# Accumulator banks of a two-layer hybrid trunk: four fixed pairs for the whole program in place of pools per stage

## The chip, the cores and the metric

One core of a Trainium2 chip runs the whole program in one launch. The metric is the device time of one execution in microseconds (us); a kernel's time is the median of its runs. The core's engines are TensorE (PE: matrix products and transposes, which write into accumulator banks), VectorE (DVE), ScalarE (ACT), GpSimd (POOL) and SyncE (SP, which issues most transfers). Each engine works through its own list of instructions in order, and engines wait for each other through semaphores that count finished instructions.

## The reference: what is computed

Two layers of a trunk over 512 latent tokens and 128 context tokens of width 1024. Cut to what matters:

```python
def _layer(x, mod, p, lam_init, ctx):
    sh1, sc1, g1, sh2, sc2, g2 = mod
    h = _rmsnorm(x, p['norm1']) * (1.0 + sc1) + sh1
    m, new_ctx = _mixer(h, p, lam_init, ctx)
    x = x + g1 * m
    h = _rmsnorm(x, p['norm2']) * (1.0 + sc2) + sh2
    x = x + g2 * _conv_ffn(h, p)
    return x, new_ctx
```

The mixer is one input projection, split among a recurrent head group (RG-LRU with convolution, gates and scans in two directions), grouped-query attention and differential attention, and one output projection over the three. The ConvFFN is an up projection to 2 x 2816 channels, a width-3 convolution, silu(g) * a, and a down projection. The conditioning rows (sh, sc, g) are products of the condition with a 1024 x 6144 matrix. A last norm follows.

## The kernel before

Every large product is made of three products of float32r parts (high by high, high by low, low by high: `mm3`, lines 347 to 350). Two kinds of loop carry them:

- `stat_mm` (line 595): weights stand still, tokens stream. One accumulator is two banks from `pb2` (line 260), one for each part of the 640 tokens, filled one after the other. The up projection (`up_pair`, 22 times a layer, two accumulators each, tile `uacc`) and the recurrent group's inputs (`lacc`) use it. Behind the second bank, `conv` copies both to SBUF with three ACT instructions (lines 1371 to 1373).
- `tok_products` (line 1302) and `proj_group` (line 617): tokens stand still, weights stream; one bank for each of five token tiles (`tacc`, `acc`). The output and down projections empty a bank by `residual`: DVE multiplies it with the gate (line 1298) and adds it to x (1299).

Smaller uses of banks: transposes of normed tokens (`nT`, `norm_b` and `norm_c`, lines 550 to 564: a token tile fills two banks, and DVE scales four blocks of the one while ACT scales four blocks of the other), of q and k (`qT`, `kT`, `dT`), gate products (`gacc`, line 706), the context's own attention (`cS`, `cPTp`), the conditioning products (`ada`, eight chunks into one bank), and in the attention stage scores (`S`), transposed probabilities (`PT`) and value products (`PV`).

Memory for accumulators is eight banks of 512 float32 a partition. Before, `psum_mode` opens pools for a stage: eight single banks (`pb`) in all stages but attention, and there three tiles of two banks (`ps`, for S and PT) and two single ones (`pb`: PV, dT, ada, adaT). At a change of stage it closes the pools and opens others on the same banks. Each call of `pb` or `ps` makes a new tile of its own, and the pool gives out its places in turn; the first instruction on a place waits for the readers of the tile that held it.

The order of the work is written by hand: the program is recorded in the order of the Python calls. `Flow` (line 55) puts small follow-up steps into the stream of products by planned times, and in the attention stage `Plan` (line 98) picks the next task by keys, planned durations and counts of free places (`ROOM`, line 104: three pairs and two single banks). Neither asks the pools; waits are added afterwards, between instructions that touch the same tile.

Of the kernel before, what the change touches and what calls it, by code (L numbers as in the profile page):

```python
# [2 lines left out]

# [8 lines left out]
F32 = mybir.dt.float32  # L12
# [204 lines left out]
def hybrid_kernel(ctx: ExitStack, tc: tile.TileContext, i, o):  # L217
# [22 lines left out]
    def tslot(name, n=644, dt=F32):  # L240
        return tp.tile([128, 644], dt, tag="t", name=name)[:, :n]

    psum, mode = ctx.enter_context(ExitStack()), {}

    def psum_mode(double, single):

        psum.close()
        for key, n in (("ps", double), ("pb", single)):
            if n:
                mode[key] = psum.enter_context(tc.tile_pool(name=key, bufs=n, space=bass.MemoryType.PSUM))  # L250

    psum_mode(0, 8)

    def ps(name, dt=F32):
        return mode["ps"].tile([128, 1024], dt, tag="ps", name=name)

    def pb(name, dt=F32):
        return mode["pb"].tile([128, 512], dt, tag="pb", name=name)

    def pb2(name, cut=CH):  # L260

# [221 lines left out]
    def ada_gen(l, u):  # L483

        acc = pb("ada")
        for k in range(KD):
            while not split_done:
                split_next()
            n = split_done.pop(0)
            for j in range(4):  # L490
                pe.matmul(acc[32 * j:32 * j + 32, :], lhsT=cc[:, k].rearrange("p a b -> p (a b)"), rhs=raws[n][:, j, :],
                          start=(k == 0), stop=(k == KD - 1), tile_position=(0, 32 * j))
            load_to(n + 2)
            if k == KD - 2:
                bias, ar, src = tslot("abias", 512), tslot("arow", 512), i["ada_b"]
                sp.dma_start(out=bias, in_=bass.AP(tensor=src.tensor, offset=src.offset + l * 6 * D + u * 2048,
                                                   ap=[[512, 4], [0, 32], [1, 512]]))
            fl.now += 1100
            yield
        dve.tensor_tensor(out=ar, in0=acc, in1=bias, op=ALU.add)  # L500
        if u:
            d = drp.tile([2, 1024], F32, tag=f"gate{u}", name=f"gate{u}")
            for j in range(2):
                r = 32 * (j + (0 if u == 1 else 2))
                sp.dma_start(out=d[:, j * 512:(j + 1) * 512], in_=ar[r:r + 2, :])
            res["g", l, u] = d
        yield
        pt = pb("adaT")
        for b in range(4):
            pe.transpose(pt[:, b * 128:b * 128 + 128], ar[:, b * 128:b * 128 + 128], ident)  # L510
        c = smp.tile([128, 2, 4, 4], F32, tag=f"cm{u}", bufs=2, name=f"cm{u}")
        for r in range(2):
            dve.tensor_copy(out=c[:, r], in_=pt.rearrange("p (b j q) -> p q j b", b=4, j=4)[:, r])
        res["c", l, u] = c.rearrange("p r j b -> p r (j b)")
# [117 lines left out]
    def mixer(l, hh, hl, first=None):  # L632
# [268 lines left out]
        def d_stack(df, dest, c0, order, jp):  # L901
# [17 lines left out]
            def out():  # L919
                for e in range(2):  # L920
                    dve.tensor_copy(out=dest[e][0:96, :, c0:c0 + 128],
                                    in_=f32(box[0][0:96, e * 256:e * 256 + 256].rearrange("p (h c) -> p h c", h=2)))
                pending[jp] -= 1

            return lo, tr, out

# [183 lines left out]
        else:  # L1110
            for m in range(2):
                lru_in(m, first[m])
        rope_tables_()
        for c in range(2):
            for d in range(2):
# [15 lines left out]
        for m in (2, 3):  # L1131
            w, acc = weights(), pb2("lacc")
            for c in range(2):
                stat_mm(acc, w, hh, hl, c, step=888)
                lru_in(m, acc, c)
        wait("a")
        wait(0)
        psum_mode(3, 2)
# [4 lines left out]
        def unit(kind, h, q):  # L1143
# [27 lines left out]
            def exp(c):  # L1171
                box["P"].append(tslot("P", T))
                act.activation(out=box["P"][c].rearrange("p (a b) -> p a b", a=2), in_=view(c), func=ACTF.Exp,  # L1173
                               bias=box["nm", c], accum_out=box["den"][:, c:c + 1])

            def recip():
                den = box["den"]
# [17 lines left out]
            def out():  # L1195
                if not e:
                    PTs[kind, p, q] = half("PT")[:, 0:1280].rearrange("p (k c) -> p k c", k=5)
                act.activation(out=PTs[kind, p, q][:, :, e * 128:e * 128 + 128],
                               in_=box["pt"][:, 0:T].rearrange("p (k c) -> p k c", k=5), func=ACTF.Copy)

            return dict(score=score, top=top, exp=exp, recip=recip, norm=norm, comb=comb, tr=tr, out=out)

        def values_of(kind, p, q):
# [19 lines left out]
            def out():  # L1223
# [4 lines left out]
                else:  # L1228
                    if not dn:
                        dn.append(v2(half("dn"), T))  # L1230
                    dst = dn[0][:, p, c0:c0 + nn]
                act.activation(out=dst, in_=box[0][:, 0:nn], func=ACTF.Copy)

            def hi():
                m = mixed[2 + p] = v2(half("mix", F32R), T)
# [257 lines left out]
    for t in range(NT):  # L1493
# [10 lines left out]
        out=cc,  # L1504
        in_=cps[:, 0:16].rearrange("p (r k) -> p k r", r=2).unsqueeze(2).to_broadcast([128, KD, 16, 2]),
    )
    rps1 = pb("rps1")
    pe.transpose(rps1[:, 0:32], rows1, ident[0:32, 0:32])
    dve.tensor_copy(out=cols1, in_=rps1[:, 0:32])
    sc1 = small("sc1", 8)  # L1510
    dve.tensor_scalar(out=sc1, in0=cols1[:, R_AB + 8:R_AB + 16], scalar1=1.0, scalar2=None, op0=ALU.add)
    act.activation(out=identr, in_=ident, func=ACTF.Copy)
# [18 lines left out]
    for g in range(2):  # L1531
# [3 lines left out]
        for e in range(2):  # L1535
            dve.tensor_copy(out=xT[2 * g + e][:, :, L:T], in_=pt[:, e * 256:e * 256 + 256].rearrange("p (k c) -> p k c", k=2))

    h = ([], [])

    def modulate(p):  # L1540
# [51 lines left out]
    for l in range(DEPTH):  # L1592
# [5 lines left out]
        if not more:  # L1598
            sps = pb("sps")
            pe.transpose(sps[0:8, 0:128], stc, ident)  # L1600
            srow = tslot("srow", 128)[0:8]
            dve.tensor_copy(out=srow, in_=sps[0:8, 0:128])
            sp.dma_start(out=o["new_lru_state"].rearrange("a l d (c p) -> (a l d c) p", p=128), in_=srow)
        ffn(l, h[0], h[1], res["g", l, 2], AB1(l + 1) if more else None, h2)
        h = h2
# [52 lines left out]
```

## Time and profile before

| | us |
|---|---|
| median of 3 runs | 1647.7 |
| lowest, highest | 1647.31, 1648.01 |
| the profiled execution | 1648.27 |
| its span, first to last instruction | 1646.5 |
| PE busy in the span | 1596.4 |
| DVE, ACT, POOL busy | 942.4, 725.4, 347.6 |

The profile is of one execution, and durations come from it. Stages by the span's time: start 0 to 47, projections of layer 0 up to 180, attention to 309, output projection and norm to 383, feed-forward to 858 (its end holds the norm before layer 1), projections of layer 1 to 989, attention to 1109, output projection and norm to 1184, feed-forward and last norm to 1646.5. Two matrix products that follow each other overlap in the records: a product of 320 columns is recorded as some 310 ns, and the next starts 150 ns after it.

### The profile page before, as it was taken

What the parts mean: (1) busy time and instruction counts of PE and PEld (TensorE: products, weight loads), DVE (VectorE), ACT (ScalarE), POOL (GpSimd) and SP (SyncE); (2) the same over time, 40 slices, a digit from 0 to 9 for tenths busy, and PEclk for the clock granted to TensorE, in tenths of its full rate; (3) what the DMA queues carried; (4) which work ended last, traced back from release to release, by engine and by line L of the source; (5) the groups of instructions that cost most, each with busy time, mean ns of one, the idle gap of its engine ahead of it and who ended that gap; (6) DMA issues with size and microseconds to landing.
All of it is one profiled execution on the core that took longest, in us unless ns stands there. A gap on an engine that the chain in (4) does not pass through costs nothing. (4 is left out here: it accounts for less than half of the span.)

```text
span 1646.5 us, 25389 instructions
## 1 busy us (share of the span) xinstructions
PE 1596.4 (97%) x10070; PEld 1395.2 (85%) x10070; DVE 942.4 (57%) x1548; ACT 725.4 (44%) x1500; POOL 347.6 (21%) x746
## 2 busy tenths in 40 slices
PE   6999999999999999999999999999999999999998
PEld 4787777789999889999887787777899998899986
DVE  5785867555555334555467677875655553345544
ACT  4745677644333212333247357784433331133321
POOL 5162243122111000111052613420411100011101
PEclk9999999999999999999999999999999999999999
DMA  9222365411312321222212214443112232121312
GB/s 330 68 89 83 128 214 202 170 52 52 103 52 92 114 77 52 78 78 78 102 36 70 80 58 134 151 141 127 41 63 77 77 128 78 45 84 52 103 65 90
DMA packets 99435, 161.04 MB, mean 98 GB/s; under 512 B 10670, under 2 KB 69222, under 8 KB 94196
## 3 DMA queue, kind: packets, MB, share of 16 engines
q1 hardware_dynamic: 98068, 158.00, 28.7%
q8 instruction: 79, 1.29, 0.3%
q0 software_dynamic: 1040, 1.14, 0.2%
q14 instruction: 40, 0.33, 0.1%
q10 hardware_dynamic: 208, 0.28, 0.0%
HBM read 155.95 MB, written 3.44 MB: 97 GB/s over the span
## 5 line engine op out<-in xcount | busy, mean ns | idle before, releaser
L334 DVE TENSOR_TENSOR wl<-raw,wh 128x1024 fp32r<-128x1024 f32 x180 | 220.5, 1231 | 414.0 <-ACT wh L333 413.0
L349 PE MATMUL uacc<-hl,wh 128*128 128x320 f32 (+2 forms) x1408 | 437.1, 310 | 0.8 <-DVE hl L578 0.5
L348 PE MATMUL uacc<-hh,wh 128*128 128x320 f32 (+2 forms) x1408 | 436.4, 310 | 0.0
L350 PE MATMUL uacc<-hh,wl 128*128 128x320 f32 (+2 forms) x1408 | 435.6, 309 | 0.2 <-DVE wl L334 0.2
L333 ACT ACTIVATE wh<-raw 128x1024 fp32r<-128x1024 f32 x180 | 189.4, 1058 | 183.6 <-PE tacc L350 148.5
L349 PEld LDWEIGHTS uacc<-hl,wh 128*128 128x128 f32 x1408 | 265.6, 189 | 1.7 <-DVE hl L578 1.6
L350 PEld LDWEIGHTS uacc<-hh,wl 128*128 128x128 f32 x1408 | 264.6, 188 | 0.8 <-DVE wl L334 0.8
L348 PEld LDWEIGHTS uacc<-hh,wh 128*128 128x128 f32 x1408 | 264.8, 188 | 0.3
L349 PE MATMUL tacc<-wl,g 128*128 128x512 f32 x440 | 173.8, 395 | 0.0
L348 PE MATMUL tacc<-wh,g 128*128 128x512 f32 x440 | 173.8, 395 | 0.0
L350 PE MATMUL tacc<-wh,g 128*128 128x512 f32 x440 | 173.2, 394 | 0.0
L1376 POOL TENSOR_SCALAR ca<-u,fcol 128x642 f32<-128x642 f32 x44 | 39.0, 887 | 416.6 <-issue 243.6
L1169 DVE TENSOR_REDUCE nm<-S 128x1 f32<-128x640 f32 x128 | 103.0, 818 | 34.8 <-PE S L1159 17.7
L1173 ACT ACTIVATE P<-S,nm 128x640 f32<-128x640 f32 x128 | 101.2, 792 | 35.3 <-DVE nm L1169 25.3
L1184 POOL TENSOR_SCALAR P<-P,den 128x640 f32<-128x640 f32 x96 | 80.2, 839 | 167.4 <-DVE den L1178 88.5
L1372 ACT ACTIVATE u<-uacc 128x192 f32<-128x192 f32 (+1 forms) x88 | 29.1, 331 | 184.7 <-PE uacc L350 184.7
L350 PEld LDWEIGHTS tacc<-wh,g 128*128 128x128 f32 x440 | 82.6, 188 | 19.7
L348 PEld LDWEIGHTS tacc<-wh,g 128*128 128x128 f32 x440 | 82.6, 188 | 19.6
L349 PEld LDWEIGHTS tacc<-wl,g 128*128 128x128 f32 x440 | 82.6, 188 | 19.0
L348 PE MATMUL acc<-wh,hh 128*128 128x512 f32 x240 | 97.4, 406 | 0.0
L349 PE MATMUL acc<-wl,hh 128*128 128x512 f32 x240 | 96.3, 401 | 0.9 <-DVE wl L334 0.9
L350 PE MATMUL acc<-wh,hl 128*128 128x512 f32 x240 | 95.6, 398 | 0.0
(291 smaller groups left out, 2673.5 us busy)
## 6 DMA issues: line engine op xcount, KB each, us to landing
raw<-in_ffn_w_up_dram SPq DMA_DIRECT2D x44, 1024.0 KB, 5.0
raw<-in_ada_w_dram SPq DMA_DIRECT2D x40, 1024.0 KB, 4.9
raw<-in_ffn_w_down_dram SPq DMA_DIRECT2D x20, 1024.0 KB, 5.0
raw<-in_w_in_dram SPq DMA_DIRECT2D x16, 1024.0 KB, 8.3
araw<-in_ada_w_dram SPq DMA_DIRECT2D x16, 512.0 KB, 9.6
raw<-in_w_out_dram SPq DMA_DIRECT2D x8, 1024.0 KB, 5.0
gates<-gate SPq DMA_DIRECT2D x8, 512.0 KB
x<-in_x_sample_dram SPq DMA_DIRECT2D x4, 512.0 KB
```

The costliest lines, as they stand in the source:

```text
L333: act.activation(out=wh, in_=raw, func=ACTF.Copy)
L334: dve.tensor_tensor(out=wl, in0=raw, in1=f32(wh), op=ALU.subtract)
L348: pe.matmul(out, lhsT=lh, rhs=rh, start=start, stop=False)
L349: pe.matmul(out, lhsT=lh, rhs=rl, start=False, stop=False)
L350: pe.matmul(out, lhsT=ll, rhs=rh, start=False, stop=stop)
L1169: dve.tensor_reduce(out=box["nm", c], in_=view(c), op=ALU.max, axis=AX.XY, negate=True)
L1173: act.activation(out=box["P"][c].rearrange("p (a b) -> p a b", a=2), in_=view(c), func=ACTF.Exp, bias=box["nm", c], accum_out=box["den"][: ...
L1184: pool.tensor_scalar(out=P[-1], in0=P[-1], scalar1=den[:, 1 + comps:2 + comps], scalar2=0.0, op0=ALU.mult, op1=ALU.add)
L1372: act.activation(out=u[:, 1 + cut:1 + L], in_=acc[1][:, 0:L - cut], func=ACTF.Copy)
L1376: pool.tensor_scalar(out=out, in0=u[:, 1:1 + n], scalar1=wcol(1), scalar2=wcol(3), op0=ALU.mult, op1=ALU.add)
```

## The change

One pool of four tiles of two banks each is opened once (`acc`), and every accumulator is a view of one of them. `pb` takes the single bank, `ps` the pair (of the first three pairs), that nobody holds and that was given out longest ago. Whether a bank is held is read from Python's count of references to its view, so the program now drops its views (`del`, `clear`, `pop`) where it has no more use for them. `psum_mode` no longer opens or closes anything; it only says whether single banks must come from the fourth pair. The diff, cut to its core; at each of the places left out a view is dropped in the same way:

```diff
-    psum, mode = ctx.enter_context(ExitStack()), {}
+    pairs_ = ctx.enter_context(tc.tile_pool(name="acc", bufs=4, space=bass.MemoryType.PSUM))
+    bank_of = [pairs_.tile([128, 1024], F32, tag="acc", name="acc") for _ in range(4)]
+    held, used, turn = [None] * 8, [0] * 8, [0]
+
+    def take(banks, ap):
+        turn[0] += 1
+        for b in banks:
+            held[b], used[b] = [ap], turn[0]
+        return ap
+
+    def idle(b):
+        return held[b] is None or sys.getrefcount(held[b][0]) <= 1 + sum(h is not None and h[0] is held[b][0] for h in held)
+
+    def ps(name):
+        p = min((p for p in range(3) if idle(2 * p) and idle(2 * p + 1)), key=lambda p: max(used[2 * p:2 * p + 2]))
+        return take((2 * p, 2 * p + 1), bank_of[p][:, 0:1024])
+
+    def pb(name, dt=F32):
+        free = [b for b in range(8) if idle(b)]
+        if paired[0]:
+            free = [b for b in free if b >= 6]
+        b = min(free, key=lambda b: used[b])
+        ap = bank_of[b // 2][:, b % 2 * 512:b % 2 * 512 + 512]
+        return take((b,), ap.bitcast(dt) if dt != F32 else ap)
+
+    paired = [False]
 
     def psum_mode(double, single):
-
-        psum.close()
-        for key, n in (("ps", double), ("pb", single)):
-            if n:
-                mode[key] = psum.enter_context(tc.tile_pool(name=key, bufs=n, space=bass.MemoryType.PSUM))
-
-    psum_mode(0, 8)
-
-    def ps(name, dt=F32):
-        return mode["ps"].tile([128, 1024], dt, tag="ps", name=name)
-
-    def pb(name, dt=F32):
-        return mode["pb"].tile([128, 512], dt, tag="pb", name=name)
+        paired[0] = double > 0
...
         dve.tensor_tensor(out=ar, in0=acc, in1=bias, op=ALU.add)
+        del acc
...
                                bias=box["nm", c], accum_out=box["den"][:, c:c + 1])
+                del box["s", c]
...
-                act.activation(out=dst, in_=box[0][:, 0:nn], func=ACTF.Copy)
+                act.activation(out=dst, in_=box.pop()[:, 0:nn], func=ACTF.Copy)
```

Each engine's list holds the same instructions in the same order; what differs is the tile that each bank belongs to, and the waits. In the rows below, the number behind a name tells tiles apart: `acc_83` to `acc_86` are the four pairs, and the names in brackets are the engines whose semaphores an instruction waits for. Lines after the change are some 17 to 24 higher.

On PE at the start, where normed tokens (`xn`) are transposed, four to a bank, before:

```order
L1526 MATMUL xTp_223<-ident_90,xn_190 128x128 [waits DVE_49]
L1526 MATMUL xTp_229<-ident_90,xn_160 128x128
L1526 MATMUL xTp_229<-ident_90,xn_170 128x128
L1526 MATMUL xTp_229<-ident_90,xn_180 128x128
L1526 MATMUL xTp_229<-ident_90,xn_190 128x128
```

And now:

```order
L1550 MATMUL acc_84<-ident_94,xn_192 128x128 [waits DVE_49]
L1550 MATMUL acc_84<-ident_94,xn_162 128x128 [waits DVE_49]
L1550 MATMUL acc_84<-ident_94,xn_172 128x128
L1550 MATMUL acc_84<-ident_94,xn_182 128x128
L1550 MATMUL acc_84<-ident_94,xn_192 128x128
```

The second four go to the other bank of the same pair, and the first of them waits for DVE, which copies the first four.

On PE in a down projection of layer 0, where the products of one token tile end and those of the next begin, before:

```order
L348 MATMUL tacc_5806<-wh_5929,g_5822 128x512
L349 MATMUL tacc_5806<-wl_5930,g_5822 128x512
L350 MATMUL tacc_5806<-wh_5929,g_5822 128x512
L348 MATMUL tacc_5814<-wh_5895,g_5444 128x512
L349 MATMUL tacc_5814<-wl_5896,g_5444 128x512
```

And now:

```order
L364 MATMUL acc_86<-wh_5590,g_5483 128x512
L365 MATMUL acc_86<-wl_5591,g_5483 128x512
L366 MATMUL acc_86<-wh_5590,g_5483 128x512
L364 MATMUL acc_86<-wh_5556,g_5118 128x512 [waits DVE_49]
L365 MATMUL acc_86<-wl_5557,g_5118 128x512
```

The new token tile's bank is the mate of the one just filled, and its first product waits for DVE.

On ACT in the norm before the feed-forward of layer 1, where it scales its half of the transposes (`nT`), the second to the fourth token tile, before:

```order
L562 ACTIVATE hf_11591<-nT_11581,cm1_10314,A2_11521 128x128 [waits PE_49]
L562 ACTIVATE hf_11591<-nT_11581,cm1_10314,A2_11521 128x128 x3
L562 ACTIVATE hf_11657<-nT_11647,cm1_10314,A2_11521 128x128 [waits PE_49,Pool_49]
L562 ACTIVATE hf_11657<-nT_11647,cm1_10314,A2_11521 128x128 x3
L562 ACTIVATE hf_11723<-nT_11713,cm1_10314,A2_11521 128x128 [waits PE_49,Pool_49]
```

And now:

```order
L579 ACTIVATE hf_10930<-acc_86,cm1_9758,A2_10863 128x128 [waits DVE_49] x4
L579 ACTIVATE hf_10993<-acc_85,cm1_9758,A2_10863 128x128 [waits PE_49,Pool_49]
L579 ACTIVATE hf_10993<-acc_85,cm1_9758,A2_10863 128x128 x3
L579 ACTIVATE hf_11056<-acc_84,cm1_9758,A2_10863 128x128 [waits PE_49,Pool_49]
L579 ACTIVATE hf_11056<-acc_84,cm1_9758,A2_10863 128x128 x3
```

Where both banks of a token tile belong to one pair (`acc_86`), each of ACT's four instructions waits for DVE, which reads the other bank.

## Rows read from the trace of the kernel before

**Rows 1.** The page, part 1: busy time, share of the span, instructions.

```profile
PE 1596.4 (97%) x10070; PEld 1395.2 (85%) x10070; DVE 942.4 (57%) x1548; ACT 725.4 (44%) x1500; POOL 347.6 (21%) x746
```

**Rows 2.** Busy time by stretch: stretch, length, busy by engine, then clock, DMA share, GB/s.

```profile
0.00:47.00 47.00, 30.02 (x256) 22.54 (x257) 27.10 (x63) 21.08 (x42) 21.50 (x52) 1.00 0.97 315
47.00:180.40 133.40, 124.73 (x634) 102.14 (x632) 98.74 (x226) 76.12 (x176) 44.81 (x58) 0.99 0.20 65
...
858.00:989.00 131.00, 124.02 (x633) 101.81 (x632) 93.57 (x193) 73.49 (x168) 46.00 (x62) 0.99 0.22 68
```

**Rows 3.** Timeline, up projection: start, length, engine, line, operation, tiles, count.

```profile
415.58 0.31 PE L348 MATMUL uacc<-hh,wh 128*128 128x320 f32 x1
...
415.73 0.31 PE L349 MATMUL uacc<-hl,wh 128*128 128x320 f32 x1
...
416.01 0.27 ACT L1373 ACTIVATE u<-uacc 128x128 f32<-128x128 f32 x1
```

**Rows 4.** Timeline, down projection of layer 0, a change of token tile.

```profile
582.14 0.40 PE L348 MATMUL tacc<-wh,g 128*128 128x512 f32 x1
...
582.34 0.69 DVE L1298 TENSOR_TENSOR res<-tacc,gates 128x512 f32<-128x512 f32 x1 [1.37 <-PE tacc L350]
```

**Rows 5.** Timeline, output projection of layer 0 with the norm behind it.

```profile
363.13 1.03 PE L553 MATMUL nT<-ident,xn 128*128 128x128 f32 x8
...
364.36 0.68 DVE L1298 TENSOR_TENSOR res<-tacc,gates 128x512 f32<-128x512 f32 x1
...
377.36 0.42 PE L348 MATMUL uacc<-hh,wh 128*128 128x384 f32 x1
...
379.31 1.36 DVE L564 TENSOR_SCALAR hf<-nT,A,cm 128x128 f32<-128x128 f32 x4
```

**Rows 6.** Timeline, gate products of layer 0 (PE: two products in the row).

```profile
58.08 0.70 PE L706 MATMUL gacc<-lruG,lruW 128*128 128x320 f32 x2
...
58.01 1.07 ACT L707 ACTIVATE lruR<-gacc,cols 128x320 f32<-128x320 f32 x2 [1.93 <-PE gacc L706]
```

**Rows 7.** Timeline, context attention among projections, layers 0 and 1.

```profile
164.92 0.41 PE L348 MATMUL lacc<-hh,wh 128*128 128x320 f32 x1
...
168.83 0.20 ACT L1047 ACTIVATION_READ_ACCUMULATOR cP<-cS,cnm 128x1 f32 x1
...
973.52 0.41 PE L348 MATMUL lacc<-hh,wh 128*128 128x320 f32 x1
...
978.11 0.21 ACT L1047 ACTIVATION_READ_ACCUMULATOR cP<-cS,cnm 128x1 f32 x1
```

**Rows 8.** Timeline, attention: the first score products, and one later transpose.

```profile
180.46 0.61 PE L1158 MATMUL S<-kk,qa 128*128 128x320 f32 x1 [2.05 <-DVE dks L921]
...
989.05 0.54 PE L1158 MATMUL S<-kk,qa 128*128 128x320 f32 x1 [2.06 <-DVE dks L921]
...
1053.34 1.15 PE L1193 MATMUL PT<-ident,P 128*128 128x128 f32 x6
...
1054.19 0.20 ACT L1173 ACTIVATION_READ_ACCUMULATOR P<-S,nm 128x1 f32 x1
```

**Rows 9.** Timeline, attention: a score product that waits for a pair.

```profile
186.21 0.20 ACT L1173 ACTIVATION_READ_ACCUMULATOR P<-S,nm 128x1 f32 x1
...
186.46 0.41 PE L1158 MATMUL S<-kk,qa 128*128 128x320 f32 x1 [0.52 <-ACT P L1173]
186.71 0.31 PE L1159 MATMUL S<-kl,qa 128*128 128x320 f32 x1
```

**Rows 10.** Timeline, the start: DVE's copies of transposes, PE's wait for weights.

```profile
14.71 1.46 DVE L1530 COPY xT<-xTp 128x512 f32<-128x512 f32 x2
...
24.18 1.07 PE L1545 MATMUL ada<-araw,cc 128*32 128x256 f32 x16 [1.78 <-DMA araw<-in_ada_w_dram]
```

**Rows 11.** Busy time by stretch, right behind two stops of PE; clock third from last.

```profile
180.20:183.60 3.40, 3.14 (x14) 3.10 (x15) 1.77 (x4) 0.77 (x1) 0.00 (x0) 0.51 0.00 0
...
989.20:992.50 3.30, 3.30 (x14) 3.23 (x15) 1.65 (x2) 1.15 (x1) 0.00 (x0) 0.50 0.02 5
```

More of the change, by code (lines that the diff above doesn't have):

```diff
@@ L1 @@
 import math
+import sys
 from contextlib import ExitStack
@@ L923, in out @@
                 pending[jp] -= 1
+                box.clear()
             return lo, tr, out
@@ L1112, in mixer @@
                 lru_in(m, first[m])
+        del first[:]
         rope_tables_()
@@ L1135, in mixer @@
                 lru_in(m, acc, c)
+        del acc
         wait("a")
@@ L1199, in out @@
                                in_=box["pt"][:, 0:T].rearrange("p (k c) -> p k c", k=5), func=ACTF.Copy)
+                del box["pt"]
             return dict(score=score, top=top, exp=exp, recip=recip, norm=norm, comb=comb, tr=tr, out=out)
@@ L1506, in hybrid_kernel @@
     )
+    del cps
     rps1 = pb("rps1")
@@ L1509, in hybrid_kernel @@
     dve.tensor_copy(out=cols1, in_=rps1[:, 0:32])
+    del rps1
     sc1 = small("sc1", 8)
@@ L1536, in hybrid_kernel @@
             dve.tensor_copy(out=xT[2 * g + e][:, :, L:T], in_=pt[:, e * 256:e * 256 + 256].rearrange("p (k c) -> p k c", k=2))
+    del pt
     h = ([], [])
@@ L1602, in hybrid_kernel @@
             dve.tensor_copy(out=srow, in_=sps[0:8, 0:128])
+            del sps
             sp.dma_start(out=o["new_lru_state"].rearrange("a l d (c p) -> (a l d c) p", p=128), in_=srow)
```

## The prediction

> **What bounds the kernel now.** I read the busy line first: TensorE (PE) is busy 97% of the span, no other engine over 57% [rows 1]. So a microsecond in which PE newly waits is nearly a microsecond of time, and a new wait on another engine costs only what reaches PE. Next I read the stages, to see how much idle PE has that could swallow a delay: 8.7 us in the projections of layer 0 (133.40 less 124.73) 7.0 us in those of layer 1 (131.00 less 124.02), 17 us at the start [rows 2]. Then I looked at each place where PE hands an accumulator over and goes on with the next one: the timeline gives the start of PE's next product and the end of the copy that empties the accumulator.
>
> **What the change does to order and waits.** Every engine runs the same instructions in the same order; no transfer moves. What differs is which bank a product gets, and the waits. Before, each bank is a tile of its own. After, there are four tiles of two banks, and the order with its waits shows a wait between two instructions on different engines as soon as both touch the same *pair*, whichever bank each uses: the fifth transpose of xTp waited for nothing and now waits for VectorE (DVE), the next token tile's product now waits for DVE, and the copies of nT, halves of one pair read by ScalarE (ACT) and DVE, take turns. I followed every wait of PE in both programs to the instruction that fulfils it and looked that one up in the trace: in 132 places PE now waits for something that in the trace of before ends only after PE's own start. Those shortfalls, with 0.05 us of hand-over each (ACT ends at 186.41, PE starts at 186.46 [rows 9]), add up to 138 us if all are charged in full. By stage:
>
> *The feed-forward stages and their down products (33 places).* In the up projection PE starts a new accumulator at 415.58 while ACT still copies the last one until 416.28 [rows 3]. Where the new bank and the old one are mates, PE waits for that copy: 0.70 + 0.05 = 0.75 us. That holds for one accumulator in four, 22 in all, because the order of use falls out of step with the pairs. In the down product PE starts at 582.14, and the DVE multiply on the token tile before ends at 583.03 [rows 4]: 0.94 us, 9 times. With two more places of these stages (0.70 and 1.89 us): 27.6 us. These copies follow directly on PE's own last product, so a delay of PE delays them as well, and every one of these waits is paid again; I charge them in full.
>
> *The output projections with the norm of the next stage (16 places).* Two of the worst are PE at 363.13 against the DVE multiply that ends at 365.04, and PE at 377.36 against DVE's copies that end at 380.67 [rows 5]: 2.0 and 3.4 us; a third is 2.6. Layer 1 repeats the pattern. Shortfalls: 13.7 + 13.4 = 27.0. About 2 us of idle go, and the copies that now take turns add about as much, so 27.
>
> *The projections (33 and 14 places).* Gate products: the second of the row starts at 58.35 (0.43 before its end), and the ACT copy of its mate ends at 59.08 [rows 6]: 0.78, seven times. Where the short attention on context tokens is woven in, waits come in bunches and overlap: PE at 164.92 would wait for ACT's exponentials that end at 169.03, PE at 973.52 for those that end at 978.32 [rows 7]. In the first bunch (157 to 165 us, seven waits) the sum is 13.8 and the largest alone 4.2; in the second (968 to 974, six waits) 17.8 and 4.9. Each later wait is measured from a PE that is already late, so the sum is too much; the ACT copies wait in part for PE's late products, so the largest is too little. I take 6 and 9. Three smaller bunches, 12.3 in sum, become 6.3. That makes 37.1 - 7.8 - 4.1 = 25.2 and 26.8 - 8.8 - 1.9 = 16.1; PE's idle swallows some 2 and 1.6 of it: 23.2 and 14.5.
>
> *The attention stages (11 and 19 places).* Least recently *taken* is not longest *free*: PE's transposes get a pair that ACT has just finished reading. In the row at 1053.34 the second transpose, which opens a new pair at 1053.75, waits for ACT, which ends at 1054.39 [rows 8]: 0.69 us. Shortfalls 4.7 + 8.6 = 13.2. Here something is also given back: before, the first score product of each layer stood idle for 2.05 and 2.06 us until DVE had emptied the last bank of the closing pools [rows 8]; the pairs it gets now are free. That leaves 9.1. The value products now share a pair with the running conditioning product, so ACT's and DVE's copies come later by up to 1.8 us, and later steps with them; the trace does not price this, 0 to 9 us; I take 4: 13.
>
> *The start (6 places).* Each bank's four transposes wait for the DVE copy of its mate, 0.73 us apiece (1.46 for two) and 0.6 to 1.9 with the way there: 6.5. PE waits there for weights anyway, 1.78 us at 24.18 [rows 10] and 1.5 in two more rows, so 3.2 remains.
>
> Sum of waits: 27.6 + 27 + 23.2 + 14.5 + 13 + 3.2 = 108.5 us.
>
> *Getting going again.* After a wait that holds the weight load too, the second product starts 0.25 us behind the first (186.46, 186.71), against 0.15 in the run before a wait (415.58 to the next row at 415.73) [rows 3, 9]. About 120 of the 132 waits really stop PE: 0.1 x 120 = 12. If the weights are in already, 0.
>
> *The clock.* After the 2.05 us stop at 180.46 the granted clock is 0.51 for 3.4 us, the lower level of 1.2 GHz [rows 8, 11]; so a drop costs some 1.7 us of products. It is the same behind the stop at 989.05 (0.50), while the start keeps 1.00 through its 1.78 us stop [rows 2, 10]. Seven of the new waits are over 2 us, and two old ones of that size go: 5 x 1.7 = 8.5 us, between 0 and 25 (if all fifteen stops from 1.5 us up drop it).
>
> Total: 108.5 + 12 + 8.5 = 129 on top of the profiled run's own 1648.3, which is 0.6 above the median of 1647.7. I predict a median of **1777 us**.
>
> **Rivals.** (1) *Banks stay independent.* If the chip's waits on a mate's copy were already met when PE comes, only the gain at the attention's start is left: 2.05 + 2.06 less what falls due next, so 1644 us, faster. For it: before, copies and products on neighbouring banks run at the same time without harm [rows 3]. Against it: the waits stand in the program, and 132 of them ask for work that the trace shows unfinished. It decides from 4 us of new waits downward. The Trainium skill, "PSUM — Partial Sum Buffer", section "PSUM bank collisions raise a hardware error", speaks for this side: engines clash only on the same bank, so guarding each bank by itself is enough. By that rule no wait between mates is needed, and the change would give about those 1644 us; but the rule tells what the chip needs, and the order shows that more is guarded here.
> (2) *Delays hide each other.* While PE stands, ACT and DVE catch up, and only the largest wait of each bunch counts, with no cost of getting going and no more clock drops than before: 27.6 (feed-forward) + 23 (norms) + 13 and 6 (projections, all their idle of rows 2 used up) + 4 = 74, so 1722 us. For it: ACT is busy 44% [rows 1]. Against it: most releasers follow on PE's own last product.
> (3) *Bunches in full and a slow clock.* The bunches charged in full (+22) and every stop from 1.5 us up at half clock (+17): 1816 us. For it: where the engines feed each other, a delay goes round. Against it: the clock held through the 1.78 us stop.
> (4) *The waits are there and fall almost all into slack*, so nothing is left to measure: 1648 us. Against it: 97% busy.
>
> **How the numbers follow.** Forecast 76%, rival 1 3%, rival 2 10%, rival 3 9%, rival 4 2%. The forecast's own bounds are the start-up cost (0 to 13), the clock (0 to 25), the bunches and the attention term; its low end is 1777 - 12 - 8 - 9 - 8 = 1740, its high end with rival 3 is 1820. The range 1740 to 1820 holds some 80%. A measurement of this kernel can tell about 0.2%, 3.3 us, from no change: slower by more than that 95% (forecast, rivals 2 and 3), within it 2% (rival 4), faster 3% (rival 1).
>
> **What will show it.** PE's idle before each kind of product: about 0.75 us before one new up accumulator in four, released by ACT's last copy; 0.94 before one token product in three or so, released by the DVE multiply; 2 to 4 us at the norms; the 2 us before the first score product gone. DVE's and ACT's own busy times should stay as they are, as should transfers. PE's busy share should fall to about 90%. I am wrong in the sizes if the idle is there but bunches differ, and wrong in the mechanism if PE still starts next to a running copy in the mate bank.

## The result: slower, 1783.3 us

| | before | after |
|---|---|---|
| median of the runs | 1647.8 us | 1783.3 us (1778.8 to 1785.1) |
| profiled execution, span | 1648.3, 1646.5 us | 1778.8, 1777.1 us |
| PE busy, share of the span | 1596.4 us, 97% | 1637.5 us, 92% |

The ratio is 1.0819, between 1.0797 and 1.084 with 95%. The forecast was 1777 us, 1740 to 1820. The profiled execution is the shortest of the four; its clock was 0.984 on average, that of the two longest (1784.7 and 1785.1 us) 0.977 and 0.980.

The page of the changed kernel, part 1: busy time, share of the span, instructions (answers [rows 1]).

```profile
PE 1637.5 (92%) x10070; PEld 1410.0 (79%) x10070; DVE 944.7 (53%) x1548; ACT 728.0 (41%) x1500; POOL 342.7 (19%) x746
```

ACT and DVE do the same work in the same busy time. PE's busy time grew by 41 us although it does the same products too: that is products stretched by the lower clock and by starting again after a stop, and the part of each stop that the record of the product ahead still covers. The other 89 us are idle.

Busy time by stage of the changed kernel, each stage cut where its first product starts (answers [rows 2]; columns as there, the clock third from last).

```profile
0.00:55.80 55.80, 35.00 (x256) 26.03 (x257) 26.75 (x63) 20.85 (x42) 20.98 (x52) 0.97 0.86 274
55.80:216.20 160.40, 135.33 (x635) 106.28 (x633) 98.31 (x223) 76.73 (x176) 43.38 (x58) 0.94 0.15 51
216.20:350.50 134.30, 125.84 (x1195) 90.15 (x1193) 93.17 (x202) 95.65 (x206) 44.79 (x59) 1.00 0.57 195
350.50:441.90 91.40, 77.97 (x349) 62.96 (x349) 45.05 (x77) 36.63 (x74) 17.25 (x33) 0.96 0.21 69
441.90:932.30 490.40, 477.10 (x2828) 442.26 (x2827) 232.66 (x280) 153.90 (x297) 62.36 (x208) 1.00 0.22 74
932.30:1075.60 143.30, 127.76 (x634) 104.16 (x632) 91.67 (x188) 72.84 (x166) 44.58 (x62) 0.96 0.19 62
1075.60:1205.10 129.50, 118.74 (x1128) 88.39 (x1126) 92.83 (x201) 95.22 (x206) 44.12 (x59) 1.00 0.40 135
1205.10:1297.60 92.50, 79.38 (x356) 63.83 (x355) 44.84 (x78) 37.12 (x75) 16.82 (x33) 0.96 0.20 69
1297.60:1777.10 479.50, 460.39 (x2709) 425.96 (x2707) 219.41 (x241) 139.09 (x259) 48.45 (x183) 0.99 0.22 75
```

Set against the same stages before, every one is longer. In the table the clock column is the time that products lost or won because one of the two traces has them at the lower clock, found by matching PE's products one to one; the rest is idle and restart. The clock is read from the trace's records of it, which begin at 16.31 us before and at 29.94 after the change; what it cost ahead of them stands in the rest of the start, 3.5 us (see the start, below).

| stages | forecast of waits | growth measured | of it the clock | the rest |
|---|---|---|---|---|
| start | 3.2 | 8.8 | 1.4 | 7.4 |
| projections, layer 0 | 23.2 | 26.9 | 6.1 | 20.8 |
| attention, both layers | 13 | 15.6 | -2.5 | 18.1 |
| output projection and norm, both | 27 | 34.7 | 6.5 | 28.2 |
| feed-forward, both | 27.6 | 32.3 | 2.2 | 30.1 |
| projections, layer 1 | 14.5 | 12.3 | 2.8 | 9.5 |
| sum | 108.5 | 130.6 | 16.5 | 114.1 |

The waits view of PE in the changed kernel (us in total, times, longest) names the releasers; the first four rows:

```profile
PE acc L364 <- ACT u L1395: 12.9, 22, 0.6
PE acc L364 <- DVE res L1320: 10.3, 13, 0.9
PE acc L570 <- DVE res L1320: 9.8, 4, 4.0
PE acc L364 <- ACT hf L579: 6.3, 3, 2.3
```

L364 is the first product of an accumulation (L348 before), L1395 the last copy out of an up accumulator, L1320 the multiply on a token tile, L570 a transpose of a normed tile, L579 ACT's copy of one. The 22 and the 13 are the hand-overs that the forecast counted (22 up accumulators, 9 down products and four of the output projections).

One up hand-over in the timeline of the changed kernel, beside [rows 3]:

```profile
474.35 0.31 PE L366 MATMUL acc<-hh,wl 128*128 128x320 f32 x1
...
474.92 0.27 ACT L1395 ACTIVATE u<-acc 128x128 f32<-128x128 f32 x1
...
475.25 0.42 PE L364 MATMUL acc<-hh,wh 128*128 128x320 f32 x1 [0.59 <-ACT u L1395]
...
475.50 0.31 PE L365 MATMUL acc<-hl,wh 128*128 128x320 f32 x1
```

PE's starts lie 0.15 apart in a run; here 0.90, then 0.25. So 0.75 are lost before the product and 0.10 behind it, 0.85 in all, while the row's bracket says 0.59: the record of the product before overlaps the wait. That is why 89 us of idle go with 131 us of time.

The down hand-over in the timeline, beside [rows 4]: PE stands until DVE's multiply ends.

```profile
645.40 0.69 DVE L1320 TENSOR_TENSOR res<-acc,gates 128x512 f32<-128x512 f32 x1 [1.37 <-PE acc L366]
...
646.14 0.50 PE L364 MATMUL acc<-wh,g 128*128 128x512 f32 x1 [0.78 <-DVE res L1320]
```

The norm in the timeline, second token tile of layer 0. In the kernel before each engine made its four copies in one row, DVE's later because DVE had other work first:

```profile
357.80 1.51 ACT L562 ACTIVATE hf<-nT,cm,A 128x128 f32<-128x128 f32 x4 [2.96 <-PE nT L553]
...
359.50 1.36 DVE L564 TENSOR_SCALAR hf<-nT,A,cm 128x128 f32<-128x128 f32 x4
```

In the changed kernel:

```profile
406.57 0.40 DVE L581 TENSOR_SCALAR hf<-acc,A,cm 128x128 f32<-128x128 f32 x1
407.01 0.46 ACT L579 ACTIVATE hf<-acc,cm,A 128x128 f32<-128x128 f32 x1 [6.49 <-DVE hf L581]
407.50 0.41 DVE L581 TENSOR_SCALAR hf<-acc,A,cm 128x128 f32<-128x128 f32 x1 [0.53 <-ACT hf L579]
407.95 0.46 ACT L579 ACTIVATE hf<-acc,cm,A 128x128 f32<-128x128 f32 x1 [0.48 <-DVE hf L581]
...
415.64 1.94 PE L570 MATMUL acc<-ident,xn 128*128 128x128 f32 x8 [4.03 <-DVE res L1320]
```

Two engines that only read, each its own bank, take turns; the eight copies last 3.7 us (406.57 to 410.28) instead of 3.1 (357.80 to 360.86). The expectation of a run below sets the 3.7 against 1.5, which is the first token tile, whose copies ran side by side. In the changed kernel the two banks come from one pair, and the copies take turns, for one of the five token tiles in the norm of layer 0 and for two in that of layer 1 (1262.75 and 1290.45); together their copies last 2.1 us longer than before.

### The profile page after: what moved, and what is told of

It reads as the page before. It is cut to its first block, busy times and chain, and to the rows that moved or that the text cites. A ratio compares the mean times of both kernels' runs of the same rounds, so it can differ in the third digit from the quotient of the medians.

```text
span 1777.1 us, 25397 instructions
## 1 busy us (share of the span) xinstructions
PE 1637.5 (92%) x10070; PEld 1410.0 (79%) x10070; DVE 944.7 (53%) x1548; ACT 728.0 (41%) x1500; POOL 342.7 (19%) x746
## 5 line engine op out<-in xcount | busy, mean ns | idle before, releaser
L364 PE MATMUL acc<-hh,wh 128*128 128x320 f32 (+2 forms) x1536 | 487.0, 317 | 28.1 <-ACT u L1395 12.9
L365 PE MATMUL acc<-hl,wh 128*128 128x320 f32 (+2 forms) x1536 | 482.8, 314 | 0.1
L366 PE MATMUL acc<-hh,wl 128*128 128x320 f32 (+2 forms) x1536 | 480.5, 313 | 0.0
L364 PEld LDWEIGHTS acc<-hh,wh 128*128 128x128 f32 x1536 | 294.1, 191 | 37.0 <-ACT u L1395 18.6
L365 PEld LDWEIGHTS acc<-hl,wh 128*128 128x128 f32 x1536 | 295.0, 192 | 0.8 <-DVE hl L1593 0.3
L366 PEld LDWEIGHTS acc<-hh,wl 128*128 128x128 f32 x1536 | 294.1, 191 | 0.3 <-DVE wl L350 0.3
L364 PE MATMUL acc<-wh,g 128*128 128x512 f32 x440 | 174.7, 397 | 8.8 <-DVE res L1320 7.1
L365 PE MATMUL acc<-wl,g 128*128 128x512 f32 x440 | 173.8, 395 | 0.0
L366 PE MATMUL acc<-wh,g 128*128 128x512 f32 x440 | 173.2, 394 | 0.0
L1189 DVE TENSOR_REDUCE nm<-acc 128x1 f32<-128x640 f32 x128 | 102.9, 819 | 37.9 <-PE acc L1183 19.6
L1205 POOL TENSOR_SCALAR P<-P,den 128x640 f32<-128x640 f32 x96 | 79.8, 834 | 182.2 <-DVE den L1199 100.5
L364 PE MATMUL acc<-wh,hh 128*128 128x512 f32 x240 | 98.9, 412 | 12.6 <-ACT da L993 2.4
L364 PEld LDWEIGHTS acc<-wh,g 128*128 128x128 f32 x440 | 82.6, 188 | 32.1 <-DVE res L1320 9.8
L366 PEld LDWEIGHTS acc<-wh,g 128*128 128x128 f32 x440 | 82.6, 188 | 19.6
L1320 DVE TENSOR_TENSOR res<-acc,gates 128x512 f32<-128x512 f32 x60 | 41.5, 691 | 94.5 <-PE acc L366 94.3
```

The costliest lines, as they stand in the source:

```text
L364: pe.matmul(out, lhsT=lh, rhs=rh, start=start, stop=False)
L365: pe.matmul(out, lhsT=lh, rhs=rl, start=False, stop=False)
L366: pe.matmul(out, lhsT=ll, rhs=rh, start=False, stop=stop)
L1189: dve.tensor_reduce(out=box["nm", c], in_=view(c), op=ALU.max, axis=AX.XY, negate=True)
L1205: pool.tensor_scalar(out=P[-1], in0=P[-1], scalar1=den[:, 1 + comps:2 + comps], scalar2=0.0, op0=ALU.mult, op1=ALU.add)
L1320: dve.tensor_tensor(out=tm, in0=acc, in1=g[r][:, hs], op=ALU.mult)
```

## Experiments

The diffs are cut to their core. They are against the changed kernel, or against the kernel before where that is said.

### Without the guard, and with the same order

```diff
- pairs_ = ...tile_pool(name="acc", bufs=4, ...)          # four tiles of two banks
- bank_of = [pairs_.tile([128, 1024], ...) for _ in range(4)]
+ bank_of[:] = [mode["pb"].tile([128, 512], ...) for _ in range(single)]   # one bank each
+ # psum_mode closes and opens pools around attention, as before
```

> Eight tiles of one bank each, handed out least recently taken first as in the changed kernel, outside the attention stages; the pools close and open around attention as in the kernel before. The order of handing out is kept, the guard by pairs is gone. Theory (the guard by pairs makes the waits): 8 of the 132 new waits of TensorE are left, all but one in the projections and 7 us in sum before idle is used up; the time comes out at 1648 to 1655 us, the idle before the up accumulators is gone, the 2.05 us before the first score product stay. Rival (the order of handing out makes the waits): the idle of about 28 us before the stationary-weight products stays, 1740 us or more.

Measured: 1650.15 us, ratio 1.0013 (1.0004 to 1.0022). The order of handing out is nearly free outside attention; with a tile for each bank, and attention's banks from pools as before, the 135 us are gone. Its PE never waits for `u`, and the stop before the scores is still there, as its waits view shows:

```profile
PE S L1180 <- DVE dks L940: 4.1, 2, 2.0
```

### A choice of banks that knows the pairs

```diff
- b = min(free, key=lambda b: used[b])
+ b = min(free, key=lambda b: (not idle(b ^ 1), max(used[b], used[b ^ 1]), used[b]))
+ # and the second bank of an accumulator is the mate of its first
```

> The changed kernel with another rule for the choice of a bank: a whole free pair that was least recently taken first, and the two banks of one accumulator from one pair. The guard by pairs stays. Theory (a wait is paid where the bank that is taken has a mate still being read, and nowhere else): 78 new waits with 74 us of shortfall are left instead of 132 with 138; none at the up accumulators and the down products, so these stages return to the lengths of before; the total follows the shortfalls, 1648 + 74 x 131/138 = 1718 us, between 1700 and 1735. Rival (the guard costs something at every hand-over, whichever bank is taken): the up and down stages stay as in the changed kernel and the time is above 1760 us.

Measured: 1721.84 us, ratio 1.0451 (1.0437 to 1.0466). The start and the last feed-forward stage are back to before within 0.8 us, so the start's 8.8 us came of the waits too. What is left stands in the projections (8.4 + 8.4), attention (6.7 + 9.7), the norms (14.6 + 15.4) and the norm at the end of the first feed-forward (8.3). The norms are dearer than PE's shortfalls there (5.8 and 5.7, counted as in the prediction). In this kernel the copies take turns for three of the five token tiles of each norm; the next run undoes that.

### The same, with the two halves of a normed tile in different pairs

```diff
- pt = pb2("nT")
+ pt = pb_apart("nT")      # the second bank from a pair other than the first's
```

> The kernel that chooses by pairs (1721.8 us), except that the two halves of a normalized token tile go to banks of different pairs. The shortfalls of TensorE's new waits are the same in sum (74.3 us against 74.0, 78 places each), but ScalarE and VectorE may now read the two halves at the same time instead of in turn. In the trace of the changed kernel eight copies in turn take 3.7 us (406.57 to 410.28), in the kernel before 1.5. Theory (copies in turn put off what follows at the norms): the stages with the output projection and the norm, +14.6 and +15.4 us in the kernel that chooses by pairs, come down by 4 to 7 us each: 1708 to 1716 us. Rival (ScalarE and VectorE have room, turns cost nothing): 1719 to 1724.

Measured: 1704.03 us, ratio 1.0347 (1.0331 to 1.0362): 18 us less for the same shortfalls of PE, and below the 1708 to 1716 that were expected. In the profiled executions the norms fell from 14.6 to 8.1 and from 15.4 to 8.2 us, within the 4 to 7 us each or just above; the norm at the end of the first feed-forward, which the expectation left out, fell from 8.3 to 4.7. The timeline of this kernel has the first tile's copies side by side, where they lasted 3.8 us in the run before (367.91 to 371.69):

```profile
370.21 1.37 DVE L597 TENSOR_SCALAR hf<-acc,A,cm 128x128 f32<-128x128 f32 x4
370.22 1.50 ACT L595 ACTIVATE hf<-acc,cm,A 128x128 f32<-128x128 f32 x4 [5.00 <-DVE A L560]
```

The Trainium skill ("PSUM — Partial Sum Buffer", section "Specifications (TRN2)") says that ScalarE and VectorE read that memory at the same time at full speed as long as they don't meet on a bank. These rows agree: 1.50 and 1.37 us side by side, and 1.51 (357.80) and 1.36 (359.50) with the other engine elsewhere in the kernel before.

### The price of one hand-over, made larger

```diff
  act.activation(out=u[:, 515:515 + S], in_=acc[1][:, L - cut:T - cut], func=ACTF.Copy)
+ for _ in range(2):       # 4 in the next two runs; the third is an edit of the kernel before
+     act.activation(out=u[:, 1 + cut:1 + L], in_=acc[1][:, 0:L - cut], func=ACTF.Copy)
+     act.activation(out=u[:, 515:515 + S], in_=acc[1][:, L - cut:T - cut], func=ACTF.Copy)
```

> The changed kernel with ScalarE's two copies out of the second bank of each up accumulator done three times instead of once (the same values to the same place). Two copies start 0.41 us after each other's start in the changed kernel's trace, so the last one ends 0.82 us later. Theory (TensorE waits for the last copy at 22 hand-overs): the idle before these grows from 0.6 to about 1.4 us, 22 x 0.82 = 18 us on top of the changed kernel's 1783: 1801 us, between 1796 and 1812, more if stops of 1.4 us lower the clock. Rival (ScalarE's copies are not what these hand-overs cost): 1780 to 1788.

> The same with five times instead of once, 1.64 us later at the end. Theory: idle of about 2.2 us at 22 hand-overs, 36 us more than the changed kernel: 1819 us with the clock at 1.00 in the feed-forward stages. A stop of 2.05 us was followed by a drop of the clock in the kernel before, at 180 and 989 us: if each of the 22 stops costs one (1.7 us), another 37: 1856. The range for both is 1812 to 1862. Rival (the copies are not the cause): 1780 to 1790.

> Control: the same five-fold copies in the kernel before, where the next product's bank is a tile of its own. Theory (without the guard by pairs a longer copy is hidden): 1646 to 1652 us, no idle before the up accumulators. Rival (88 x 1.64 = 144 us more work on ScalarE shows by itself, in the gating steps or the next weights): 1660 us or more, and then the two runs before can't be read as the price of the hand-over.

Measured: 1797.56 (ratio 1.0911, 1.089 to 1.0932), 1827.66 (1.1099, 1.1076 to 1.1121), and the control 1648.61 (1.0007, 0.9997 to 1.0016). The row of the waits view that was 12.9, 22, 0.6 reads, with two and with four extra rounds:

```profile
PE acc L364 <- ACT u L1398: 30.1, 22, 1.4
```

```profile
PE acc L364 <- ACT u L1398: 49.4, 23, 2.5
```

The first adds 17.2 us at 22 places, 0.78 each where 0.82 was expected; the time grew by 14. The second adds 36.5 us (22 longer stops and one of 0.8), and its feed-forward stages are 50.8 us longer than those of the changed kernel: 39.2 of idle, 9.9 of lower clock, the rest restart. In the control ScalarE is busy 134 us more (859.7 against 725.4), and no more than 2.6 us of them show. Both theories of the second run hold in part: the clock fell behind 7 of its 22 longer stops (21 of 2.16 to 2.49 us and one of 1.90), not behind none and not behind all. The timeline at one that it fell behind, and the stretches behind a stop that it held through and behind this one:

```profile
538.67 0.41 PE L364 MATMUL acc<-hh,wh 128*128 128x320 f32 x1 [2.16 <-ACT u L1398]
```

```profile
475.70:479.00 3.30, 3.30 (x22) 3.30 (x23) 2.37 (x3) 0.86 (x1) 0.98 (x4) 1.00 0.06 3
540.00:543.30 3.30, 3.30 (x14) 3.30 (x13) 2.50 (x3) 0.67 (x1) 0.00 (x0) 0.50 0.33 104
```

Both stops were 2.16 us long (the other one stands before 475.68). Behind them PE issued 22 products in 3.3 us at 1.00, and 14 at 0.50. What stood ahead was alike: a stop of 0.49 us some 9.5 us earlier (466.17 and 529.18), and products without a gap since.

### Attention alone, whole and in halves

```diff
  # pools as before in all other stages
+ bank_of[:] = [pairs_.tile([128, 1024], ...) for _ in range(4)]    # first run: pairs for scores and for single banks
+ # second run: score pairs from a pool as before, the two single banks are one pair
+ # third run: score pairs least recently taken first, the single banks from a pool as before
```

> Pools as in the kernel before, except that the attention stages open one pool of four pairs and take from it as the changed kernel does. Theory (each stage pays its own price): in the changed kernel's trace the two attention stages are 6.1 and 9.5 us longer although 2.05 and 2.06 us of stops and two drops of the clock (2.6) had gone; here the stops and the drops stay, so 15.6 + 4.1 + 2.6 = 22 us more: 1670 us, between 1662 and 1678. By the prediction's own shortfalls (4.7 + 8.6) it is 1661. Rival (the attention stages are longer in the changed kernel only because of what runs into them from the projections): 1648 to 1654.

> Half of the change in the attention stages alone (e2_attn_pairs, 1666.9 us, +19): the three score pairs come from a pool as in the kernel before, and only the two single banks are the halves of one pair. New waits of TensorE: 9 places, 3.9 us of shortfall. The prediction put 0 to 9 us on this sharing beside the shortfalls and took 4. Theory (sharing and order are separate prices that add up, 4 + 4 here): 1652 to 1658 us. Rival (the sharing makes nearly all of the 19 us, because the values' copies hold up the conditioning product and the other way round): 1660 to 1667.

> The other half: the score pairs are handed out least recently taken first, the two single banks come from a pool of their own as in the kernel before. No tile has a mate that others use. New waits: 21 places, 9.4 us of shortfall, all on ScalarE's exponentials. Theory (least recently taken is not longest free, so TensorE gets a pair that is still being read; each delay comes back through the chain of scores, exponentials and transposes): 1657 to 1663 us, and this and the sharing add up to about the 19 us of both. Rival (the order costs nothing without sharing, as outside attention, where eight single banks in the same order measured 1.0013): 1646 to 1651.

Measured: 1666.93 us (ratio 1.0117, 1.0104 to 1.0131), 1658.1 (1.0066, 1.0049 to 1.0082), 1656.67 (1.0057, 1.0042 to 1.0072). The whole costs 19.3 us and the halves 10.6 and 9.2: they add up. Attention pays for itself, and the order of handing out, nearly free elsewhere, costs here. The text ahead of the prediction says that a pool gives its places out in turn; the banks that the kernel before got in attention (first banks 0, 4, 2, 0, 4, 2, 2, 0, 4 for the first nine score and transpose tiles) are not in turn. Least recently taken picks others, and PE meets pairs that ACT still reads. The waits view of the order run, where the kernel before has 1.8 us for scores and no row of this kind for transposes (L1215):

```profile
PE acc L1179 <- ACT P L1194: 3.1, 7, 0.6
PE acc L1215 <- ACT P L1194: 3.0, 6, 0.9
```

The sharing run fell outside its 1652 to 1658 by little, and the order run below its 1657 to 1663 by as little. The sharing run's shortfalls were only 3.9 us, so some 7 us came by another way than PE's own waits for a mate. Which of the later steps carry them isn't settled.

### A wider guard

```diff
- bank_of = [pairs_.tile([128, 1024], ...) for _ in range(4)]
+ bank_of = [pairs_.tile([128, 2048], ...) for _ in range(2)]    # the same banks, guarded by four
```

> The changed kernel with two tiles of four banks in place of four of two. Every product gets the same bank as in the changed kernel; only the guard is wider. 314 places with 278 us of shortfall instead of 132 with 138; in the up projections every second accumulator waits instead of every fourth (44 places in place of 22), and 70 + 60 places in attention instead of 11 + 19. Theory (the price follows the shortfalls that the guard makes, 131/138 of them): 1648 + 278 x 0.95 = 1912 us, between 1870 and 1980, as attention's chains may give back more or less. Rival (the waits of one place hide in those of another once there are many): 1800 to 1850.

Measured: 2005.16 us, ratio 1.2166 (1.2148 to 1.2184). The waits view:

```profile
PE acc L364 <- ACT u L1395: 32.5, 42, 1.3
PE acc L364 <- DVE res L1320: 20.4, 26, 0.9
```

Twice as many hand-overs wait in the up and in the down products, as counted, and the two feed-forward stages grew by 79.8 us for 60 us of shortfall. Attention grew by 66 and 71 us where its shortfalls are 31 and 26. There a delay of PE delays the exponentials that PE waits for next, so shortfalls read from the undisturbed trace are far too small. The clock is part of it: with PE's products matched as above it makes 47 us of the whole, 17 of them in attention. The rival is refuted; the theory's size is 93 us short of what was measured, outside its range.

### Keeping what the change was to give

```diff
+ two = ctx.enter_context(tc.tile_pool(name="two", bufs=2, ...))     # open for the whole program
  # the pool of the other six banks is closed for attention and opened again behind it
+ if b and (name == "dT" or not a or count[0] % 3 == 0):             # a, b: places left in the six, in the two
+     key, pool_ = "two", two
```

> The kernel before with two of its eight single banks in a pool that stays open for the whole program; only the pool of the other six is closed for attention. Every bank is a tile of its own. The last transposes of the delta keys go to the two kept banks, so that the first score product no longer waits for their copies. Theory (the stop before the first score product is a cost of closing the pool, and the drop of the clock behind it is a cost of the stop): 2.05 + 2.06 us of stops go, 0.60 + 0.48 before the first token products behind attention go, the granted clock stays at 1.00 behind 178 and 987 us (1.35 + 1.24 us); one new wait of 0.5: 1640 to 1642 us. Rival (what is due next, DVE's maxima of the first scores, takes the gain back): 1645 to 1648 us.

Measured: 1645.05 us, ratio 0.9982 (0.9973 to 0.9991), 2.6 us below the kernel before. The first score product starts right behind the transposes (179.37), and the clock stays up behind it:

```profile
179.37 0.38 PE L1179 MATMUL S<-kk,qa 128*128 128x320 f32 x1
```

```profile
178.00:182.00 4.00, 2.81 (x24) 2.34 (x23) 3.56 (x11) 0.44 (x1) 0.00 (x0) 1.00 0.00 0
```

Of the 7 us that the theory gave, 2.6 are there: the rival holds for the greater part. What is due next is the exponentials, not DVE's maxima that the rival named. The waits view has, where the kernel before shows 4.1 us for the stops and 1.8 us in 4 waits on `P`:

```profile
PE S L1179 <- ACT P L1194: 4.3, 6, 1.5
```

Waits of the delta transposes on DVE grew from 0.4 to 1.8 us as well, and behind 995 us the clock is down once.

## Why the prediction held

**The mechanism** was right: the three kinds of wait that it named are there at the places and in the numbers that it named, the stop before the first scores is gone, and with the guard by single banks the new waits go (1.0013). Rival 1 fell on what the prediction had against it: the chip doesn't need a wait between mates, as the kernel of single banks shows by running without, but the program holds one. Its 1644 us are what the kernel with two kept banks gives (1645). Rival 2 was right that the delays in a bunch hide each other, wrong that starting again and the clock cost nothing; of rival 3 the slow clock came in the main, the bunches in full did not.

**The feed-forward term**, 27.6 and 33 restarts of 0.1, measured 30.1 without the clock: 0.75 lost before the product and 0.10 behind it, as forecast. Raising ACT's copies moved it by 0.78 us a place.

**The norms**, 27, measured 28.2 without the clock. The prediction held the copies in turn to cost about 2 us, and the three tiles that take turns last 2.1 us longer. Where three tiles of each norm take turns, the comparison of the two kernels that choose by pairs makes turns 6.5 and 7.2 us of a norm stage, so what hangs on them costs more than their own length; how much that is in the changed kernel wasn't tried. PE's stop at 363.13 of the trace of before became 4.03 us where 2.0 was forecast, and that at 377.36 became 3.11 where 3.4 was.

**The bunches in the projections** were taken at 6 and 9 us instead of 13.8 and 17.8. PE's idle there is 5.2 (0.54, 1.71, 1.36 and 1.62) and 6.2 (2.68, 1.19, 2.32). With the clock taken out, PE's products around them grew apart by 5.0 and 6.4 us (156.5 to 166.5 and 967.5 to 975 of the trace of before). So delays in a bunch do hide each other, more than the prediction took, and the two projection stages with restarts came to 30.3 instead of 37.7 plus restarts.

**Attention** was forecast at 13 with 4 for the value products' pair; it grew by 15.6 although the clock gave back 2.5. Alone, it costs 19.3 against 13.2 of shortfalls. The prediction saw that least recently taken is not longest free; the run on the order puts 9.2 us on that, for shortfalls of 9.4. The sharing, 10.6 for shortfalls of 3.9, is 6.7 dearer than its shortfalls where the prediction took 4 of 0 to 9. The switch's stop is gone, as said: the first score product starts without a wait.

**The start** is the step that failed: 3.2 forecast, 8.8 measured. The waits themselves did not fail. PE's five stops between transposes (1.72, 0.79, 0.79, 0.78 and 0.92 us) took 6.4 us with their restarts, where 6.5 was said; and the waits for weights did swallow delay, 3.1 us by 25.83 of the trace of before and 1.7 later. Two terms were put at nothing. The first is the clock. Below are 32 products in the kernel before, then the same 32 and the next 32 in the changed one:

```profile
18.91 1.93 PE L1545 MATMUL ada<-araw,cc 128*32 128x256 f32 x32
```

```profile
27.46 3.13 PE L1570 MATMUL acc<-araw,cc 128*32 128x256 f32 x32
...
31.54 1.93 PE L1570 MATMUL acc<-araw,cc 128*32 128x256 f32 x32
```

PE starts the program at half the pace, as at the lower of its two clock levels. Before, transposes stood 0.21 us apart until 16.4 us, when PE had gone on without a stop since 13.25, and 0.11 from there. In the changed kernel it stopped five times until 26.41; transposes still stood 0.21 apart and the products behind them 0.43, and these came down to 0.21 at 29.98. The transposes and products that ran at the lower pace only now lost 3.5 us. (The clock column shows 1.00 there, as its records begin only where the pace rises, so [rows 2] did not show the lower pace.) In the kernel that chooses by pairs, without these stops, the pace rises at 16.8. The second is ACT's late copy:

```profile
35.09 1.04 ACT L349 ACTIVATE wh<-raw 128x1024 fp32r<-128x1024 f32 x1
...
36.04 0.36 ACT L1573 ACTIVATE arow<-acc 128x256 f32<-128x256 f32 x1
...
36.46 0.44 PE L1576 MATMUL acc<-ident,arow 128*128 128x128 f32 x2 [2.99 <-ACT arow L1573]
```

Before, this copy ran as soon as PE was done (27.04), and PE stood 0.58. Now the transposes ahead are late, DVE's scaling is late, and ACT's copy stands in its queue behind two roundings that wait for DVE and one of weights. That is 2.4 us more, and a drop of the clock behind the stop (36.8 to 40.2), 1.4 in the table. I had looked at PE's waits alone.

**The clock**, 8.5 us for five more drops, measured 16.5 in the profiled execution, and 20.0 with the 3.5 at the start. The term was mis-sized: only stops above 2 us were counted, each for one drop of 3.4 us. In the changed kernel 12 stretches between the start and the last products are at 0.5 (4 in the kernel before), three of them 6.8 us long; two stand behind stops of 1.71 and 1.74, others behind two shorter ones in a row (0.69 and 0.95 ahead of 142.6; 1.32 and 0.69 ahead of 917.4). Two of these stretches, behind those two shorter stops and behind the 4.03 of the norm, in the view by stretch (beside [rows 11]):

```profile
142.60:146.00 3.40, 3.40 (x8) 2.72 (x9) 1.73 (x5) 0.00 (x0) 3.23 (x8) 0.50 0.90 286
...
415.70:419.00 3.30, 3.30 (x12) 2.99 (x13) 1.89 (x5) 1.33 (x4) 0.00 (x0) 0.50 0.00 0
```

So the waits and restarts were forecast at 120.5 and came to 110.6 (114.1 less the start's 3.5), the clock at 8.5 and came to 20.0. The two errors cancel in the total of 130.6 against 129: that it came so close is in part luck. The median is 4.5 us above the profiled execution, in runs whose mean clock is lower.

## What to carry to other kernels

Before banks are joined in one tile, list every pair of neighbours in time that would share it: the guard is as wide as the tile, and it binds readers to readers as well as writers to readers. Price such a wait by the end of the work it would wait for against the start that the trace shows; that holds where the releaser follows on the waiter's own last product, is too much in a bunch, and far too little where the engines feed each other in a loop. When a step is moved late, look at the queue of the engine that does it next, not only at the engine that waits, and at whether PE still reaches its higher clock as early.

## What the chip showed that was not expected

- Stops of equal length don't act alike on TensorE's clock. Behind 2.05 and 2.06 us before the first scores the kernel before ran at 0.51 and 0.50 [rows 11]; behind 2.04 and 2.03 us at the same place the kernel of single banks ran at 1.00, as its view by stretch shows:

```profile
179.40:183.00 3.60, 3.33 (x24) 2.19 (x24) 2.38 (x4) 1.81 (x2) 0.00 (x0) 1.00 0.00 0
```

  Of the 22 stops at up accumulators in the kernel with four extra rounds (1.90 to 2.49 us) 7 were followed by a drop to 0.50; of the 22 of 0.6 us in the changed kernel and the 22 of 1.2 to 1.4 us with two extra rounds, none. Within the changed kernel two stops of 2.33 us at the same product of layers 0 and 1 (399.35 and 1253.97) differ too: none behind the first, a drop to 0.50 behind the second. What decides between equal stops was not tried.
- The number of drops differs between runs of one kernel, and the time goes with it: of the changed kernel's four, the shortest (1778.8) has the mean clock 0.984, the longest (1785.1) 0.980 and the next (1784.7) 0.977.
